# The last unit's weight sums in a scratch buffer, and one weight block split by VectorE instead of by an accumulating DMA

## The chip, the cores and the metric

The kernel runs on one core of one Trainium2 chip. The metric is the device time of one execution in microseconds (us). The core's engines are TensorE (PE, matmuls; its weight loads are listed as PEld), VectorE (DVE), ScalarE (ACT), GpSimd (POOL) and SyncE (SP, which only issues transfers here). POOL issues transfers too, above all those that add to their destination.

## What is computed

One layer of a decoder trunk on 1024 prompt tokens and 8 sample tokens (1032 columns), model width 1024: a mixer with pooling and convolution, cross attention, and a gated feed-forward block with 22 tiles of 128 hidden channels. The change lies in the last step, the down projection and the final norm:

```python
    h = rmsnorm(x, g_ffn)
    x = x + (jax.nn.silu(h @ w_gate) * (h @ w_up)) @ w_down
...
        y_prompt = rmsnorm(xp, g_final)
```

## The kernel before, around the change

**Two parts per factor.** Every matmul operand is kept as a high part and a low part, and each product is three passes (high by high, high by low, low by high). ScalarE, or GpSimd, makes the high part. The low part is made in one of two ways. In `split` (line 365) VectorE subtracts the high part from the raw tile. In `split_by_dma` (line 390) ScalarE writes the negated high part, and a transfer issued by GpSimd adds the raw data from memory to it a second time. The table `BY_DMA` (line 49) names the weight blocks that take the second way.

**The down projection.** The first 16 hidden tiles go through a scheme with seven products per 2x2 block (Strassen's, in Winograd's form). They make 4 chunks, and every chunk works on 4 pairs of output rows: 16 units, numbered `u` = 0 to 15 (`down(u)`, line 1538). A unit has seven products: three of 512 columns on plain weights `dW` (6 matmuls each), and four of 520 columns on weight sums `dV` (12 matmuls of 260 columns each). `dn_load(u)` (line 1490) fetches the unit's raw weights into a tile `dr`. `dn_prep(u)` (line 1494) forms four sums of quarters of `dr` in a tile `dt` (256 columns each, line 1506, on VectorE or GpSimd), splits `dt` into `dV`, and splits parts of `dr` into `dW`. The results are added to the residual `x2` and to partial sums `pp` by VectorE (line 1339). `second_half` (line 1575) combines them by VectorE at line 1347.

**The last six hidden tiles** (16 to 21) are multiplied plainly. `hidden_load` (line 1583) fetches each into a scratch tile `ht` and splits it by DMA into `ho`. The weights come as six blocks, in this order (line 415): `w_dn` 16, `w_dn2` 0, `w_dn` 17, `w_dn` 18, `w_dn2` 1, `w_dn` 19, each through a raw tile `raw` into `w`. `last_down(c, n)` (line 1648) makes the eight output tiles `fd` of a span `c` of columns, by 18 matmuls per tile and 512 or 2x260 columns: four hidden tiles with a `w_dn` block, then two with a `w_dn2` block. `fd_0` and `fd_1` use `w_dn` 16 and `w_dn2` 0, `fd_2` and `fd_3` use `w_dn` 17 and `w_dn2` 0, and so on.

**Buffers.** Raw tiles (`dr`, `dt`, `raw`) share 3 buffers with the tag `raw`; `ht` and other scratch tiles share 3 buffers with the tag `scr`; `w` has 2, and `op` has 19. A tile takes a buffer only when the last reader of its former tile is done.

**The order.** `Program.order` (line 146) sets it: a list planner with a cost for every task takes, again and again, the engine that can start first, and the task of highest priority that is ready there and has its buffers. What it decides is written out as one fixed sequence per engine. So a buffer's tag can change which task comes first on every engine.

Of the kernel before, what the change touches and what calls it, by code (L numbers as in the profile page):

```python
# [14 lines left out]
P = 128  # L15
D = 1024
# [30 lines left out]
)  # L47

BY_DMA = {"w_in": (3, 4, 6, 7, 9, 10, 11), "w_k": (2, 3, 5, 6), "w_o": (4, 5, 6), "w_out_a": (1,), "w_out_b": (3,), "w_q": (4, 5, 6), "w_v": (0, 7), "w_dn": (17, 18, 19), "w_dn2": (1,)}
WIDE = ("w_k", "w_v")  # L50
LEAD = {"w_k": 2, "w_v": 3, "w_out_a": 15, "w_q": 15, "w_in": 1, "w_out_b": 12, "w_o": 8}
LAST_SPANS = ((0, 512), (512, 260), (772, 260))
# [28 lines left out]
CHUNKS, FIRST_LAST = 4, 16  # L81
# [22 lines left out]
class Program:  # L104
# [10 lines left out]
    def add(self, engines, emit, r=(), w=(), lock=False, func=None, nbytes=0):  # L115
        t = Task()
        t.engines = {}
        for e, cost in engines.items():
            factor, more = self.margin.get(e, (1, 0)) if not nbytes else (1, 0)
            t.engines[e] = cost * factor + more  # L120
        t.emit, t.lock, t.func, t.nbytes = emit, lock, func, nbytes
        t.prio = len(self.tasks) + self.later
        if "PE" not in engines and any(isinstance(x[0], Buf) and x[0].tag in ("mm", "ms") for x in r):
            t.prio += BIAS["evac"]
        deps = set()
        for x in r:
            if x in self.writer:
                deps.add(self.writer[x])
        for x in w:
            if x in self.writer:  # L130
                deps.add(self.writer[x])
            deps.update(self.readers.get(x, ()))
        for x in r:
            self.readers.setdefault(x, []).append(t)
        for x in w:
            self.writer[x], self.readers[x] = t, []
        deps.discard(t)
        t.deps, t.followers, t.ends = deps, [], {}
        t.waiting = len(deps)
        for d in deps:  # L140
            d.followers.append(t)
        t.bufs = list({id(x[0]): x[0] for x in list(r) + list(w) if isinstance(x[0], Buf)}.values())
        self.tasks.append(t)
        return t
# [116 lines left out]
def hybrid_step_kernel(ctx: ExitStack, tc: tile.TileContext, io):  # L261
# [11 lines left out]
    def buf(name, tag, shape, dtype=F32):  # L273
        return Buf(name, tag, shape, dtype)

    def op_buf(name, shape=(P, 2, T), dtype=F32):
        return buf(name, "op", shape, dtype)

    def op_r(name, shape=(P, 2, T)):
        return buf(name, "op", shape, F32R)  # L280

    def scr(name, shape=(P, T)):
        return buf(name, "scr", shape)
# [26 lines left out]
    def dve(n):  # L310
        return 0.065 + 0.00105 * n

    def pool_tt(n):
        return 0.14 + 0.00216 * n
# [50 lines left out]
    def split(dst, key, src, n, r, gain=None, ps=False):  # L365

        hi = {"ACT": act(n, ps, gain is not None)}
        if not ps and not state.get("alone"):
            hi["Pool"] = pool_ts(n)

        def emit_hi(e):
            if e is nc.scalar:
                e.activation(dst(0), src(), AF.Copy, scale=1.0 if gain is None else gain)  # L373
            else:
                e.tensor_scalar(dst(0), src(), 1.0 if gain is None else gain, 1.0, ALU.mult, ALU.mult)

        add(hi, emit_hi, r, [key(0)])
        lo = {"DVE": dve(n)}
        if gain is None and not ps and not state.get("alone"):
            lo["Pool"] = pool_tt(n)  # L380

        def emit_lo(e):
            if gain is None:
                e.tensor_tensor(dst(1), src(), f32(dst(0)), ALU.subtract)  # L384
            else:
                e.scalar_tensor_tensor(dst(1), src(), gain, f32(dst(0)), ALU.mult, ALU.subtract)

        add(lo, emit_lo, list(r) + [key(0)], [key(1)], lock=not ps)

    def split_by_dma(dst, key, src, n, r, again, again_keys, pool_too=False):  # L390


        def scaled(e, p, src, factor):
            if e is nc.scalar:
                e.activation(dst(p), src, AF.Copy, scale=factor)
            else:
                e.tensor_scalar(dst(p), src, factor, 1.0, ALU.mult, ALU.mult)

        either = {"ACT": act(n), "Pool": pool_ts(n)} if pool_too else {"ACT": act(n)}
        add(either, lambda e: scaled(e, 0, src(), 1.0), r, [key(0)])  # L400
        add(either, lambda e: scaled(e, 1, f32(dst(0)), -1.0), [key(0)], [key(1)])
        add({"Pool": 0.6}, lambda e: e.dma_start(dst(1), again(), accum_op=ALU.add), [key(1)] + again_keys, [key(1)], nbytes=4 * P * n)
# [38 lines left out]
    def w_prep():  # L441
# [3 lines left out]
        w = buf(f"w{i}", "op" if name in WIDE or i >= len(seq) - 4 else "w", (P, 2, 1024), F32R)  # L445
        if j in BY_DMA.get(name, ()):
            split_by_dma(lambda p: w[:, p], lambda p: (w, p), lambda: raw[:], 1024, [(raw,)],
# [1021 lines left out]
    def later(work, bias="prep"):  # L1469
        pg.later = BIAS[bias]  # L1470
        work()
        pg.later = 0
# [2 lines left out]
    x2 = [op_buf(f"x2_{j}") for j in range(4)]  # L1475
    pp = [op_buf(f"pp{j}", (P, 4, TW)) for j in range(2)]
    dn_raw, dn_w, db = {}, {}, {}

    def quarter2(p, q):


        if q < 4:
            i, h = q // 2, q % 2
            return lambda sl=slice(0, HW[h]): x2[p][:, i, h * HALF + sl.start : h * HALF + sl.stop]
        return lambda sl=slice(0, TW): pp[p // 2][:, p % 2 * 2 + q - 4, sl]
# [6 lines left out]
        dma(lambda: dn_raw[u][:], lambda: io["w_dn"][u], 4 * P * D, w=[(dn_raw[u],)])  # L1492

    def dn_prep(u):
        raw, t = dn_raw[u], buf(f"dt{u}", "raw", (P, D))
        W, V = buf(f"dW{u}", "w", (P, 2, 768), F32R), op_r(f"dV{u}", (P, 2, 1024))
        dn_w[u] = W, V

        def b(half, i):
            return lambda: raw[:].rearrange("p (k i n) -> p k i n", k=4, i=2)[:, half::2, i]  # L1500

        def s(q):
            return lambda: t[:].rearrange("p (q j n) -> p q j n", q=4, j=2)[:, q]

        def minus(q, a, b, keys, op=ALU.subtract):
            add({"Pool": pool_tt(256), "DVE": dve(256)}, lambda e: e.tensor_tensor(s(q)(), a(), b(), op), keys, [(t, q)], lock=True)

        minus(0, b(0, 1), b(0, 0), [(raw,)])
        minus(2, s(0), b(1, 1), [(raw,), (t, 0)])
        minus(3, b(1, 1), b(0, 1), [(raw,)])  # L1510
        minus(1, b(1, 0), s(2), [(raw,), (t, 2)], ALU.add)
        split(lambda p: V[:, p], lambda p: (V, p), lambda: t[:], 1024, [(t, q) for q in range(4)])
        split(lambda p: W[:, p, :512].rearrange("p (k n) -> p k n", k=4), lambda p: (W, p, 0),
              lambda: raw[:].rearrange("p (k i n) -> p k i n", k=4, i=2)[:, :, 0], 512, [(raw,)])
        split(lambda p: W[:, p, 512:].rearrange("p (k n) -> p k n", k=2), lambda p: (W, p, 1), b(1, 1), 256, [(raw,)])

    def down_blocks(c, which):
        for b in which:
            n = WIDTH[b]
            t = scr(f"hs{c}_{b}", (P, 2, n))  # L1520
            again = lambda b=b, n=n: hb[c, b][:, :, :n]
            dma(lambda t=t: t[:], again, 8 * P * n, r=[("hb", c, b, j) for j in range(2)], w=[(t,)])
            o = db[c, b] = op_r(f"hb{c}_{b}", (P, 2, 2, n))
            part, key, src = (lambda p, o=o: o[:, p]), (lambda p, o=o: (o, p)), (lambda t=t: t[:])
            if c and b in DOWN_ORDER[:4]:
                split_by_dma(part, key, src, 2 * n, [(t,)], again, [("hb", c, b, j) for j in range(2)])
            else:
                split(part, key, src, 2 * n, [(t,)])
# [75 lines left out]
    for f in range(FF_TILES):  # L1604
        if f + 1 < FF_TILES:
            if f + 1 >= AHEAD:
                later(lambda: gu_load(f + 1), "load")
                later(lambda: gate_prep(f + 1))
            later(lambda: sums_prep(f + 1))
        else:  # L1610
            pg.margin = MARGINS["down"]
            later(lambda: dn_load(0), "load")
            later(lambda: dn_prep(0))
            later(lambda: down_blocks(0, DOWN_ORDER[:4]))
        if f < AHEAD:
            others(f)
        else:
            seven(f)
    later(lambda: residual_load(0))
    later(lambda: down_blocks(0, DOWN_ORDER[4:]))  # L1620
    units = 4 * CHUNKS
    for u in range(units):
        c, p = u // 4, u % 4
        if u + 1 < 4:
# [221 lines left out]
```

## Time and profile before

| what | value |
| --- | --- |
| median of 3 runs | 1228.38 us |
| lowest and highest of them | 1224.43 and 1228.46 us |
| the profiled execution, its own time | 1224.89 us |
| its span in the profile | 1223.0 us |
| granted TensorE clock over the span | 0.997 |

The profile is of one execution. Between its span and its own time lie 1.9 us outside the program's instructions. In rows of the profile, times are in us from the span's start, buffer numbers are left out of names, and `<-` after an idle time names what ended it. A line number can be that of a helper: 1323 is every product of the seven-product schemes, 384 every low part made by subtraction, 373 and 395 every high part.

### The profile page before, as it was taken

How to read it: one execution, taken by the hardware profiler on the slowest of the kernel's cores; microseconds unless marked ns; L12 is line 12 of the kernel's file. 1: busy time of each engine (PE TensorE's matmuls, PEld its weight loads, DVE VectorE, ACT ScalarE, POOL GpSimd, SP SyncE). 2: the span in 40 equal slices, each digit the busy share in tenths (PEclk: the TensorE clock that was granted, in tenths of full speed). 3: DMA queues.
4: the chain of work that ended last, by engine and by line, in shares of the span. 5: the costliest groups of instructions: out<-in, count | busy, mean ns of one | idle time of the engine just before them, and what ended most of it. 6: DMA issues, size and time to landing. Idle time of an engine off the chain costs nothing.

```text
span 1223.0 us, 19412 instructions
## 1 busy us (share of the span) xinstructions
PE 1200.1 (98%) x7720; PEld 1122.0 (92%) x7720; DVE 927.2 (76%) x1549; ACT 527.8 (43%) x722; POOL 243.3 (20%) x296
## 2 busy tenths in 40 slices
PE   8999999999999999999999999999999999999997
PEld 8999988999999979989999999999999999999786
DVE  7999999767258886679777777777867788888654
ACT  7765556455134533444222322233222365545433
POOL 3568841231111102111000000000000124332101
PEclk9999999999999999999999999999999999999998
DMA  7335678226395773421232233222313698668612
GB/s 287 86 72 114 143 210 250 105 104 194 115 294 182 240 280 103 156 104 61 104 113 79 96 113 113 105 78 96 122 70 111 217 317 239 172 183 220 155 50 90
DMA packets 60875, 181.80 MB, mean 149 GB/s; under 512 B 7857, under 2 KB 11633, under 8 KB 59505
## 3 DMA queue, kind: packets, MB, share of 16 engines
q1 hardware_dynamic: 53824, 157.92, 37.1%
q0 software_dynamic: 6960, 22.65, 10.5%
q8 instruction: 60, 0.98, 0.3%
q14 instruction: 31, 0.25, 0.1%
HBM read 146.76 MB, written 33.78 MB: 148 GB/s over the span
## 4 chain that ended last, share of the span: by engine, by line
PE 76%; DVE 4%; DMA 2%; issue 2%; ACT 1%; POOL 0%; DVEq 0%; POOLq 0%; ACTq 0%
PE pr L1323 48%; PE ps L480 7%; PE po L480 7%; PE fd L1665 5%; PE ob L480 4%; PE oa L480 3%; PE sc L1023 1%; PE pv L1081 1%; DMA w<-in_w_q 1%; DMA raw<-in_w_out_a 1%; DMA w<-in_w_dn 0%; DVE spcache_k L1120 0%; DMA spcache_k<-in_cache_k 0%; DVE oo L1086 0%; DVE pT L1067 0%
## 5 line engine op out<-in xcount | busy, mean ns | idle before, releaser
L1323 PEld LDWEIGHTS pr<-ab,wTb 128*128 128x128 f32 x1056 | 132.1, 188 | 3.6
L1323 PE MATMUL pr<-ab,wTa 128*128 128x260 f32 x1056 | 133.6, 282 | 0.0
L1323 PE MATMUL pr<-ab,wTb 128*128 128x260 f32 x1056 | 133.3, 282 | 0.0
L1323 PEld LDWEIGHTS pr<-ab,wTa 128*128 128x128 f32 x1056 | 130.7, 189 | 2.0 <-DVE su L1339 0.3
L1323 PE MATMUL pr<-ab,wG 128*128 128x512 f32 x528 | 128.8, 392 | 0.0
L1339 DVE TENSOR_TENSOR su<-pr,su 128x520 f32<-128x520 f32 (+1 forms) x112 | 77.5, 694 | 57.5 <-PE pr L1323 57.3
L480 PE MATMUL ps<-xop,w 128*128 128x344 f32 x720 | 114.1, 320 | 0.0
L480 PEld LDWEIGHTS ps<-xop,w 128*128 128x128 f32 x720 | 113.6, 188 | 0.0
L1323 PEld LDWEIGHTS pr<-ab,wG 128*128 128x128 f32 x528 | 96.3, 188 | 18.8
L1323 PEld LDWEIGHTS pr<-hb,dV 128*128 128x128 f32 x768 | 98.4, 188 | 5.8 <-ACT dV L373 0.9
L1323 PE MATMUL pr<-hb,dV 128*128 128x260 f32 x768 | 100.2, 283 | 1.0 <-DVE dV L384 0.5
L480 PE MATMUL ps<-xq,w 128*128 128x344 f32 x576 | 94.8, 321 | 0.3 <-DMA w<-in_w_q 0.3
L480 PEld LDWEIGHTS po<-oo,w 128*128 128x128 f32 x576 | 90.9, 188 | 0.6 <-DVE oo L1086 0.4
L480 PE MATMUL po<-oo,w 128*128 128x344 f32 x576 | 91.4, 320 | 0.0
L480 PEld LDWEIGHTS ps<-xq,w 128*128 128x128 f32 x576 | 90.7, 188 | 0.7 <-DMA w<-in_w_q 0.6
L684 DVE SCALAR_TENSOR_TENSOR cacc<-glu,vec,cacc 128x511 f32<-128x511 f32 (+14 forms) x116 | 76.9, 739 | 0.0
L1323 PE MATMUL pr<-hb,dW 128*128 128x512 f32 x288 | 74.2, 394 | 0.0
L1665 PE MATMUL fd<-ho,w 128*128 128x260 f32 (+1 forms) x432 | 69.8, 322 | 0.7 <-DMA w<-in_w_dn 0.6
L1665 PEld LDWEIGHTS fd<-ho,w 128*128 128x128 f32 x432 | 61.7, 188 | 8.4 <-DMA w<-in_w_dn 1.1
L373 ACT ACTIVATE w<-raw 128x1024 fp32r<-128x1024 f32 (+1 forms) x35 | 32.9, 944 | 77.1 <-issue 19.7
L1323 PE MATMUL pr<-ab,wU 128*128 128x512 f32 x264 | 64.8, 394 | 0.0
L1350 POOL MEMSET su<- 128x16 f32 x22 | 2.5, 111 | 310.0 <-PE pr L1323 244.3
(306 smaller groups left out, 2183.9 us busy)
## 6 DMA issues: line engine op xcount, KB each, us to landing
gr<-in_w_gu SPq DMA_DIRECT2D x44, 512.0 KB, 3.6
hb<-su SPq DMA_DIRECT2D x8, 1040.0 KB, 4.6
hs<-hb SPq DMA_DIRECT2D x16, 520.0 KB, 6.7
dr<-in_w_dn SPq DMA_DIRECT2D x16, 512.0 KB, 3.7
spcache_k<-in_cache_k SPq DMA_DIRECT2D x12, 512.0 KB, 5.2
hs<-hb SPq DMA_DIRECT2D x12, 512.0 KB, 4.7
raw<-in_w_in SPq DMA_DIRECT2D x10, 512.0 KB, 3.7
hb<-he SPq DMA_DIRECT2D x8, 520.0 KB, 3.2
```

The source lines that it names most:

```text
L373: e.activation(dst(0), src(), AF.Copy, scale=1.0 if gain is None else gain)
L480: e.matmul(ps[:, c, :CW], w[:, wi, cols], x[:, xi, c * CW : (c + 1) * CW], start=first and p == 0, stop=last and p == 2)
L684: e.scalar_tensor_tensor(acc[h][:, n:], src[:, : HALF - n], w, acc[h][:, n:], ALU.mult, ALU.add)
L1023: e.matmul(bank()[:, i * NMEM : (i + 1) * NMEM], qop[2 * h + dt][:, qi, tt * P : (tt + 1) * P], kk[:, ki, 2 * (h % 2) + dt], start=(dt == ...
L1081: e.matmul(ps[:, c], v[:, vi, m, col : col + P], pT[h][m][:, pi, sl], start=(m == 0 and p == 0), stop=(m == 1 and p == 2))
L1323: e.matmul(bank(c), w[:, wi, cols(j)], xs[0](j, xi)[:, c * n : (c + 1) * n], start=onto is None and j == 0 and p == 0, stop=j == nj - 1 an ...
L1339: from_sums(sums, "DVE", dve, lambda e, src, sl: e.tensor_tensor(as_banks(o(sl), src), src, as_banks(a(sl), src), op), [akey], [okey])
L1350: add({"Pool": 0.12}, lambda e: e.memset(o(), 0.0), [], keys)
L1665: e.matmul(view(i), w[:, wi, col : col + P], hops[k][:, xi, half, lo - half * HALF + i * width // count : lo - half * HALF + (i + 1) * wid ...
```

## The change

Three edits. The block `w_dn` 17 leaves the table `BY_DMA`, so its low part is made by VectorE (`split`) and not by a negated copy and an adding transfer (`split_by_dma`). The sums `dt` of the last unit, `u` = 15, take a scratch buffer instead of a raw one. The line `units = 4 * CHUNKS` moves up, and all lines behind it are numbered one higher.

```diff
-BY_DMA = {"w_in": (3, 4, 6, 7, 9, 10, 11), "w_k": (2, 3, 5, 6), "w_o": (4, 5, 6), "w_out_a": (1,), "w_out_b": (3,), "w_q": (4, 5, 6), "w_v": (0, 7), "w_dn": (17, 18, 19), "w_dn2": (1,)}
+BY_DMA = {"w_in": (3, 4, 6, 7, 9, 10, 11), "w_k": (2, 3, 5, 6), "w_o": (4, 5, 6), "w_out_a": (1,), "w_out_b": (3,), "w_q": (4, 5, 6), "w_v": (0, 7), "w_dn": (18, 19), "w_dn2": (1,)}
...
     dn_raw, dn_w, db = {}, {}, {}
+    units = 4 * CHUNKS
...
     def dn_prep(u):
-        raw, t = dn_raw[u], buf(f"dt{u}", "raw", (P, D))
+        raw, t = dn_raw[u], scr(f"dt{u}", (P, D)) if u == units - 1 else buf(f"dt{u}", "raw", (P, D))
...
     later(lambda: down_blocks(0, DOWN_ORDER[4:]))
-    units = 4 * CHUNKS
+
     for u in range(units):
```

The planner answers with another order near the end; up to unit 12 the engines' sequences stay as they were. Three places matter later.

On TensorE, from the first product of unit 15 (`dW_10685` before, `dW_10689` now; `dV_10841` and `dV_10621` are its sums, `w_10805` and `w_10817` before are `w_dn` 16 and `w_dn2` 0). Before:

```order
L1323 MATMUL pr_10784<-hb_4_10066,dW_10685 128x512 x6
L1323 MATMUL pr_10797<-hb_2_10419,dW_10685 128x512 x6
L1323 MATMUL pr_10784<-hb_0_10183,dW_10685 128x512 x6
L1665 MATMUL fd_1_10821<-ho_10491,w_10805 128x512 x3
L1665 MATMUL fd_1_10821<-ho_10512,w_10805 128x512 x3
L1665 MATMUL fd_1_10821<-ho_10698,w_10805 128x512 x3
L1665 MATMUL fd_1_10821<-ho_10599,w_10805 128x512 x3
L1665 MATMUL fd_1_10821<-ho_10766,w_10817 128x512 x3
L1665 MATMUL fd_1_10821<-ho_10791,w_10817 128x512 x3
L1323 MATMUL pr_10856<-hb_3_10096,dV_10841 128x260 x12
```

Now:

```order
L1323 MATMUL pr_10790<-hb_4_10066,dW_10689 128x512 x6
L1323 MATMUL pr_10802<-hb_3_10096,dV_10621 128x260 x12
L1323 MATMUL pr_10820<-hb_5_10285,dV_10621 128x260 x12
L1323 MATMUL pr_10790<-hb_0_10183,dW_10689 128x512 x6
L1323 MATMUL pr_10849<-hb_6_10401,dV_10621 128x260 x12
L1323 MATMUL pr_10865<-hb_2_10419,dW_10689 128x512 x6
L1323 MATMUL pr_10876<-hb_1_10430,dV_10621 128x260 x12
L1666 MATMUL fd_0_10896<-ho_10504,w_10786 128x512 x3
```

Unit 15's four products on sums stood behind `fd_1`, and now they stand among its plain products, with all of `fd` behind them. `fd_0` and `fd_1` then run in turns: four hidden tiles each with `w_dn` 16, then two each with `w_dn2` 0 (`w_10890`).

On GpSimd, the last sums and adding transfers before:

```order
L402 DMA ho_10599<-hd 128x1040
L402 DMA ho_10698<-hd 128x1040
L402 DMA ho_10766<-hd 128x1040
L402 DMA ho_10791<-hd 128x1040
L1506 TENSOR_TENSOR dt_10819<-dr_10526,dt_10819 128x256
L402 DMA w_10869<-in_w_dn 128x1024
L402 DMA w_10906<-in_w_dn 128x1024
L402 DMA w_10925<-in_w_dn 128x1024
L402 DMA w_10945<-in_w_dn 128x1024
```

Now:

```order
L1507 TENSOR_TENSOR dt_10568<-dr_10520 128x256
L1507 TENSOR_TENSOR dt_10568<-dt_10568,dr_10520 128x256
L1507 TENSOR_TENSOR dt_10568<-dr_10520,dt_10568 128x256
L402 DMA ho_10517<-hd 128x1040
L402 DMA ho_10599<-hd 128x1040
L402 DMA ho_10702<-hd 128x1040
L402 DMA ho_10797<-hd 128x1040
L402 DMA ho_10816<-hd 128x1040
L402 DMA w_10873<-in_w_dn 128x1024
L402 DMA w_10910<-in_w_dn 128x1024
L402 DMA w_10930<-in_w_dn 128x1024
```

GpSimd makes three sums of unit 15 (`dt_10568`) where it made one (`dt_10819`). They stand ahead of the second hidden tile's adding transfer instead of behind the sixth's, and the four adding transfers for weights are three.

On VectorE, now, from the sixth product of unit 12 (`pr_10559`) on; `dr_10520` is the raw tile of unit 15, `dt_10541` holds the sums of unit 14:

```order
L1339 TENSOR_TENSOR x_0_9109<-pr_10559,x_0_9109 128x512
L1507 TENSOR_TENSOR dt_10568<-dr_10520 128x256
L1347 TENSOR_TENSOR x_0_9109<-x_0_9109 128x512
L1339 TENSOR_TENSOR x_0_9109<-pr_10572,x_0_9109 128x520
L1339 TENSOR_TENSOR x_1_9087<-pr_10592,x_1_9087 128x512
L1347 TENSOR_TENSOR x_0_9109<-x_0_9109,pp_9095 128x512
L384 TENSOR_TENSOR dV_10570<-dt_10541,dV_10570 128x1024
```

Before, VectorE's three sums of unit 15 stood far behind this, after the low part of `w_dn` 16. Now its one sum of `dr_10520` stands ahead of the first result of unit 13 (`pr_10592`).

## The prediction, written before the changed kernel had run

> **What bounds the kernel now.** First the page's busy times.
>
> ```profile
> span 1223.0 us, 19412 instructions
> PE 1200.1 (98%) x7720; PEld 1122.0 (92%) x7720; DVE 927.2 (76%) x1549; ACT 527.8 (43%) x722; POOL 243.3 (20%) x296
> ```
>
> TensorE is busy 98% of the span, so no edit that leaves its work alone can gain more than its waits. Next TensorE's timeline near the end, from unit 14 on, since the change acts there:
>
> ```profile
> 1122.08 3.06 PE L1323 MATMUL pr<-hb,dV 128*128 128x260 f32 x24
> 1124.97 1.56 PE L1323 MATMUL pr<-hb,dW 128*128 128x512 f32 x6
> ...
> 1130.64 4.32 PE L1323 MATMUL pr<-hb,dW 128*128 128x512 f32 x18
> 1134.79 4.75 PE L1665 MATMUL fd<-ho,w 128*128 128x512 f32 x18
> 1140.02 0.76 PE L1323 MATMUL pr<-hb,dV 128*128 128x260 f32 x4 [0.49 <-ACT dV L373]
> 1141.28 5.57 PE L1323 MATMUL pr<-hb,dV 128*128 128x260 f32 x44 [0.51 <-DVE dV L384]
> 1146.69 4.79 PE L1665 MATMUL fd<-ho,w 128*128 128x512 f32 x20
> 1152.12 10.22 PE L1665 MATMUL fd<-ho,w 128*128 128x512 f32 x43 [0.63 <-DMA w<-in_w_dn]
> ```
>
> In its brackets three waits are named, of 0.49, 0.51 and 0.63 us. These are too short, because the modelled end of a matmul covers part of each, so I measure them by the starts. Without a wait, 18 matmuls of 512 columns go from 1130.64 to 1134.79, or 0.2306 us each, and 24 of 260 go from 1122.08 to 1124.97, or 0.1204 us each. At these rates `fd_1` would end at 1134.79 + 18 x 0.2306 = 1138.94, but the next start is at 1140.02: 1.08 lost. Four matmuls lead to 1140.50, the next is at 1141.28: 0.78. Then 44 lead to 1146.58, the next is at 1146.69: 0.11. Then 20 lead to 1151.30, the next is at 1152.12: 0.82. Together **2.79 us** are lost between the start of unit 15 and `fd_2`.
>
> The timeline of all engines tells what was late:
>
> ```profile
> 1134.21 1.22 DVE L384 TENSOR_TENSOR w<-raw,w 128x1024 fp32r<-128x1024 f32 x1
> ...
> 1137.07 1.81 POOL L1506 TENSOR_TENSOR dt<-dr,dt 128x256 f32<-128x256 f32 x1 [5.21 <-issue]
> 1137.07 1.21 DVE L384 TENSOR_TENSOR w<-raw,w 128x1024 fp32r<-128x1024 f32 x1
> 1138.21 1.23 DVE L1347 TENSOR_TENSOR x<-x,pp 128x520 f32<-128x520 f32 x1
> ...
> 1138.91 5.20 SPq L359 DMA_DIRECT2D raw<-in_w_dn  x4
> 1138.91 1.06 ACT L373 ACTIVATE dV<-dt 128x1024 fp32r<-128x1024 f32 x1 [2.86 <-POOL dt L1506]
> 1140.00 1.23 DVE L384 TENSOR_TENSOR dV<-dt,dV 128x1024 fp32r<-128x1024 f32 x1 [0.57 <-ACT dV L373]
> ...
> 1142.69 1.06 ACT L395 ACTIVATE w<-raw 128x1024 fp32r<-128x1024 f32 x1 [2.72 <-DMA raw<-in_w_dn]
> ...
> 1146.28 0.87 POOL L402 DMA_DIRECT2D w<-in_w_dn  x1 [7.41 <-ACT w L395]
> ```
>
> All three raw buffers were taken: unit 15's weights, `w_dn` 16, `w_dn2` 0. The sums of unit 15 could start only when the low part of `w_dn` 16 (VectorE, 1134.21 to 1135.43) freed one. Their last piece ends on GpSimd at 1138.88, and `dV`'s high and low parts follow at 1138.91 and 1140.00, each with TensorE behind it. `w_dn` 17 could be fetched only when unit 15's raw tile was free, at 1138.91. Then came its conversion (1142.69), a negated copy, and the adding transfer (1146.28), whose landing TensorE met at 1152.12.
>
> **The scratch buffer.** The edit removes this knot: the sums no longer wait for a raw buffer. They wait for unit 15's weights. SP issues these, in both orders after the third hidden tile's load is out and when the same VectorE instruction frees the buffer, at
>
> ```profile
> 1104.30 0.33 SPq L359 DMA_DIRECT2D dr<-in_w_dn  x1
> ```
>
> How long that takes beside an adding transfer is bounded by these tiles, first `raw` (SP), then `ho` (adding, GpSimd), minimum, median and maximum:
>
> ```profile
> DMA to landing us min/median/max: 4.3/5.7/7.1
> ...
> DMA to landing us min/median/max: 5.5/6.9/10.1
> ```
>
> I take 5.7, an SP transfer of the same size: the weights are there at 1110.0, with 7.1 at 1111.4, and 10.1 (1114.4) is the far end. The sums on GpSimd cost 0.73 to 1.81 each:
>
> ```profile
> L1506 POOL TENSOR_TENSOR dt<-dr x3: 732/749/1737, 1093.5 to 1106.5; 128x256 f32<-128x256 f32 x3
> L1506 POOL TENSOR_TENSOR dt<-dr,dt x3: 731/800/1808, 1096.7 to 1137.1; 128x256 f32<-128x256 f32 x3
> ```
>
> Even at 1114.4, three of 1.81, 1.06 for the high and 1.23 for the low part end at 1122.1 on their own. TensorE wants them at 1130.64 + 6 x 0.2306 = 1132.02, ten us later. So 1.08 + 0.78 + 0.11 = **1.97 us** go, if nothing else becomes late. What lies behind is due earlier than before. Unit 15 now runs without a stop, 18 x 0.2306 + 48 x 0.1204 = 9.93, to 1140.57. After 24 matmuls with `w_dn` 16 come, at 1146.10, `w_dn2` 0 and the fifth hidden tile, and at 1146.80 the sixth. `fd_2` starts at 1148.87.
>
> - *Hidden tiles five and six.* ScalarE converts them only when unit 14's last matmul frees an operand buffer, at 1130.64. Four passes of 1.06 take 4.2:
>
> ```profile
> 1100.45 1.06 ACT L395 ACTIVATE ho<-ht 128x1040 fp32r<-128x1040 f32 x1
> ```
>
>  So GpSimd issues the adding transfers at about 1132.9 and 1135.0. With the median 6.9 the second lands at 1141.9, with 10.1 at 1145.1, and it is due at 1146.80: the cover is 1.7 to 4.9 us. I take no cost.
> - *`w_dn2` 0.* ScalarE's order has its high part behind that of `w_dn` 18, whose fetch starts when `w_dn` 16 is split, near 1134.3. With 7.1 it lands at 1141.4. Then 1.06 and 1.06 on ScalarE and 1.22 on VectorE lead to 1144.8, and the low part is due at 1146.10 + 2 x 0.2306 = 1146.56. With 10.1 it comes 1.2 us late. I take none.
>
> **`w_dn` 17 by VectorE.** This removes a second pass on ScalarE like that of 1142.69 (1.06), 0.87 of GpSimd's issue, and an adding transfer that TensorE met 5.8 us after its issue. It adds one subtraction of 1.22 us to VectorE. Its raw tile is fetched before unit 15 begins, since the sums hold no raw buffer. ScalarE reaches it at about 1134.9, right behind the hidden tiles, and the low part is there near 1137.3. Due at 1148.87, it has 11 us, so the **0.82 us** at 1152.12 go too. The added 1.22 us stand in VectorE's queue ahead of two results of unit 15, the second of which (`pr_10849`) leaves the buffer that `fd_0` takes at 1140.57. TensorE ends it at 1130.64 + 12 x 0.2306 + 36 x 0.1204 = 1137.74, VectorE adds it in 0.69, by 1138.6: two us of cover. Without them the subtraction would cost up to its 1.22. The remaining three adding transfers start near 1144, and with 10.1 the first lands at 1154, due at `fd_4`, 1148.87 + 36 x 0.2306 = 1157.2.
>
> **The sum:** -1.97 - 0.82 = -2.79, nothing added. That is -2.8 us on the profiled execution's own 1224.89, or 1222.1.
>
> **A rule against it.** By the Trainium skill, page "SBUF — State Buffer", section "Who interferes with whom", a VectorE instruction with two SBUF inputs and a GpSimd instruction that reads SBUF lock each other out for a whole instruction. The trace agrees: GpSimd's sum at 1137.07 took 1.81 against 0.73, and VectorE's combination at 1138.21 took 1.23 (the one at 1112.01, quoted below, has 0.68). By this rule the three sums on GpSimd cost up to 1.1 us more each, which the ten us above cover; it raises the chance of the second rival.
>
> **The rivals.** *One of the two late pieces takes the wait's place* (hidden tile six or `w_dn2` 0). For it speaks that both chains start only after unit 14 or `w_dn` 16, against it that it takes landings of the slowest kind. Price 1.2 us: the gain shrinks to 1.6, 1223.3 on the profiled execution.
>
> *VectorE stands for unit 15's weights*, and the kernel becomes slower. Its one sum of `dr` now stands ahead of the first result of unit 13, in a stretch where VectorE has nothing to spare:
>
> ```profile
> 1090.00:1100.00 10.00, 10.00 (x68) 9.19 (x67) 9.71 (x13) 6.28 (x8) 3.88 (x4) 1.00 0.38 113
> 1100.00:1110.00 10.00, 10.00 (x69) 9.22 (x68) 8.94 (x14) 5.09 (x7) 4.00 (x5) 1.00 0.94 270
> 1110.00:1120.00 10.00, 10.00 (x69) 9.23 (x68) 9.11 (x15) 4.00 (x7) 0.87 (x1) 1.00 0.97 245
> ```
>
> (the fourth column is VectorE's busy time, the last but one the DMA share). Unit 13 starts two units of 9.93 before 1130.64, at 1110.78, and TensorE adds to that first result after 18 of its matmuls, at 1110.78 + 6 x 0.2306 + 12 x 0.1204 = 1113.61. Behind the sum VectorE has 0.34, twice 0.61 and 0.69 to do (results start 0.61 apart in 1111.40, 1112.01):
>
> ```profile
> 1111.40 0.69 DVE L1339 TENSOR_TENSOR x<-pr,x 128x520 f32<-128x520 f32 x1
> 1112.01 0.68 DVE L1347 TENSOR_TENSOR x<-x,pp 128x512 f32<-128x512 f32 x1
> ```
>
> So weights that land after 1111.36, 7.1 us after their issue, stop TensorE. The median 5.7 is clear of that, 7.1 is at the edge, and 10.1 costs 3.0. Since VectorE is busy 27.8 of 30 us here, I add half a microsecond for a locked combination (1.23 - 0.68): +3.5 - 2.8 = +0.7, 1225.6. The sign turns at a landing 9.4 us after the issue. Against it: with the order now, only one adding transfer is under way then, since the second hidden tile's stands behind the sums on GpSimd.
>
> *The change doesn't do what it says*: the scratch buffer holds back the loads of hidden tiles, and the sixth comes so late that the knot only moves. VectorE frees the sums' buffer behind the fifth result of unit 13, which ends at 1110.78 + 12 x 0.2306 + 36 x 0.1204 = 1117.88. With 0.69 and 1.23 the load goes out at 1119.8, SP's 7.1 gives 1126.9, and ScalarE can use it near 1132.8. I see little for this; of the gain only `w_dn` 17's 0.8 would be left, 1224.1.
>
> **How the numbers follow.** The forecast, all waits gone, 0.70; a late piece 0.15; VectorE's stand 0.10; the knot moves 0.05. The runs shown spread from 1224.43 to 1228.46, and the profiled execution, 1224.89, lies near their lowest, 3.5 below their median. Minus 2.8 gives 1222.1 from the one and 1225.6 from the other; nothing in the profile says where in such a spread the next median falls, so I state the middle, **1223.8**. The range goes from 1221.0, the lowest run less 2.8 and 0.6 of scatter, to 1228.0, which holds every rival but VectorE's stand reckoned from the median (1229.1). Half a per cent of 1228.38 is 6.1 us, about what a measurement of this kernel can tell from no change. Faster than that means below 1222.2: the forecast, with a median near the low end of the spread, 0.70 x 0.5 x 0.7 = 0.25, and a little for scatter, 0.28. Slower than 1234.5 takes VectorE's stand several times over, 0.04. Within it: 0.68.
>
> **What would show it.** In the profile after, TensorE's timeline should run from the first product of unit 15 to `fd_2` with no idle time named, 18 + 48 + 36 matmuls in 18.2 us. The waits for `dV` and for `w` from `w_dn` should be gone from the list, SP's fetch of `w_dn` 17 should lie before 1130, and the last GpSimd sum near 1113. A wait of TensorE near 1113, or of VectorE on `dr`, speaks for the second rival; one at 1146, for `ho` or `w`, for the first. The forecast is wrong if TensorE's waits after 1100 sum to more than 1.5 us, or if time went elsewhere than between 1100 and 1153.

## The result, and the profile after

| | changed | before |
| --- | --- | --- |
| median of 12 runs | 1221.01 us | 1224.81 us |
| lowest and highest | 1219.22 and 1224.36 us | 1222.53 and 1232.47 us |
| ratio, 95% interval | 0.9962 [0.9948, 0.9976] | |
| the profiled execution, its own time and its span | 1222.57 and 1220.7 us | 1224.89 and 1223.0 us |

The changed kernel is faster: by 3.8 us between the medians, and by the ratio 4.7 us of 1224.81, with an interval from 2.9 to 6.4. That is less than half a per cent, and clear of zero. Among the experiments' runs of the kernel before are two slow ones, of 1680.20 and 2392.16 us; the medians below hold them, the ratios do not.

The page's busy times hardly move (with 19409 instructions, 3 fewer):

```profile
PE 1196.9 (98%) x7720; PEld 1121.0 (92%) x7720; DVE 927.7 (76%) x1549; ACT 527.3 (43%) x721; POOL 242.0 (20%) x296
```

TensorE has the same 7720 matmuls in 3.2 us less of modelled busy time, and ScalarE one instruction fewer, the negated copy.

TensorE's timeline of the changed kernel, from unit 15's first product on (start, length, operation, count; a wait would stand in brackets at the end):

```profile
1131.26 1.55 PE L1323 MATMUL pr<-hb,dW 128*128 128x512 f32 x6
1132.64 3.03 PE L1323 MATMUL pr<-hb,dV 128*128 128x260 f32 x24
1135.52 1.54 PE L1323 MATMUL pr<-hb,dW 128*128 128x512 f32 x6
1136.89 1.60 PE L1323 MATMUL pr<-hb,dV 128*128 128x260 f32 x12
1138.34 1.53 PE L1323 MATMUL pr<-hb,dW 128*128 128x512 f32 x6
1139.70 1.60 PE L1323 MATMUL pr<-hb,dV 128*128 128x260 f32 x12
1141.14 37.08 PE L1666 MATMUL fd<-ho,w 128*128 128x512 f32 x174
1178.06 1.02 PE L1697 MATMUL fin_ps<-fin,ones_d 128*128 128x512 f32 x2
```

No bracket is left. `fin_ps`, the first matmul of the final norm, is in both kernels the next landmark behind the same TensorE work. Before, it stood here:

```profile
1180.39 1.02 PE L1696 MATMUL fin_ps<-fin,ones_d 128*128 128x512 f32 x2
```

From unit 15's first product to `fin_ps` I call **the stage**. It took 1180.39 - 1130.64 = 49.75 before, and takes 1178.06 - 1131.26 = 46.80 now: **2.95 us less**. The span fell by 2.3 only, because this profile reached unit 15 0.62 later, on work that the change left alone.

The other engines of the changed kernel, first VectorE's timeline:

```profile
1111.04 0.43 DVE L1507 TENSOR_TENSOR dt<-dr 128x256 f32<-128x256 f32 x1 [0.21 <-DMA dr<-in_w_dn]
1111.38 1.23 DVE L1347 TENSOR_TENSOR x<-x 128x512 f32<-128x512 f32 x1
...
1136.69 1.23 DVE L384 TENSOR_TENSOR w<-raw,w 128x1024 fp32r<-128x1024 f32 x1 [0.28 <-ACT w L373]
...
1143.11 1.23 DVE L384 TENSOR_TENSOR w<-raw,w 128x1024 fp32r<-128x1024 f32 x1
```

Then SP's and GpSimd's:

```profile
1104.96 0.33 SPq L359 DMA_DIRECT2D dr<-in_w_dn  x1
...
1125.39 0.33 SPq L359 DMA_DIRECT2D raw<-in_w_dn  x1
```

```profile
1113.30 0.73 POOL L1507 TENSOR_TENSOR dt<-dr,dt 128x256 f32<-128x256 f32 x1
...
1136.01 0.86 POOL L402 DMA_DIRECT2D ho<-hd  x1 [1.22 <-ACT ho L395]
```

Unit 15's weights were issued at 1104.96, and VectorE stood 0.21 for them, until 1111.04. The last sum ends on GpSimd at 1114.03, where it ended at 1138.88 before. `w_dn` 17 is fetched at 1125.39 and no longer at 1138.91, its low part is ready at 1137.92, and that of `w_dn2` 0 at 1144.34.

### The profile page after: what moved, and what is told of

It reads as the page before. It is cut to its first block, busy times and chain, and to the rows that moved or that the text cites. A ratio compares the mean times of both kernels' runs of the same rounds, so it can differ in the third digit from the quotient of the medians.

```text
span 1220.7 us, 19409 instructions
## 1 busy us (share of the span) xinstructions
PE 1196.9 (98%) x7720; PEld 1121.0 (92%) x7720; DVE 927.7 (76%) x1549; ACT 527.3 (43%) x721; POOL 242.0 (20%) x296
## 4 chain that ended last, share of the span: by engine, by line
PE 76%; DVE 4%; DMA 3%; issue 2%; ACT 0%; DVEq 0%; SPq 0%; ACTq 0%; POOLq 0%
PE pr L1323 47%; PE po L480 7%; PE fd L1666 6%; PE ps L480 5%; PE oa L480 4%; PE ob L480 4%; PE sc L1023 1%; DMA dr<-in_w_dn 1%; DVE spcache_k L1120 1%; DMA spcache_k<-in_cache_k 1%; PE pv L1081 1%; DMA w<-in_w_k 1%; PE kps L850 0%; DMA sbcache_k<-qd 0%; DVE oo L1086 0%
```

## The experiments

Theory A at the start: the raw buffer held by unit 15's sums made all of the loss in the stage, `w_dn` 17's late fetch too, and the scratch buffer alone gains it. Theory B: the scratch buffer gains the 1.97 us ahead of `fd_2`, and `w_dn` 17 by VectorE the 0.82 behind it, as the prediction had it. The later runs ask what covers each freed wait, and how large the gain is. Each was compared with runs of the kernel before on the same chip.

### e1_scratch_only: the scratch buffer alone

```diff
-"w_dn": (18, 19)
+"w_dn": (17, 18, 19)
```

(in `BY_DMA` of the changed kernel, so `w_dn` 17 takes the adding transfer again.)

> Sums of unit 15 in a scratch buffer, w_dn 17 still by the adding transfer. Theory A (every bit of the gain is TensorE's waits between the start of unit 15 and fd_2, and the raw buffer alone caused them all, since w_dn 17 is fetched some 14 us earlier when the sums hold no raw buffer): as the full change, no wait of TensorE there, -2.9 us against before, and 89.4 us from unit 15's first product to the end of the span. Theory B (the sum of the prediction, each edit its own term): -2.0, with a wait of about 0.8 for w_dn 17 left in front of fd_2, 90.3 us.

Median 1222.37 beside 1225.12, ratio 0.9966 [0.9946, 0.9986]. TensorE's timeline, and GpSimd's issue for `w_dn` 17:

```profile
1134.47 1.55 PE L1323 MATMUL pr<-hb,dW 128*128 128x512 f32 x6
...
1144.36 37.08 PE L1666 MATMUL fd<-ho,w 128*128 128x512 f32 x174
1181.28 1.02 PE L1697 MATMUL fin_ps<-fin,ones_d 128*128 128x512 f32 x2
```

```profile
1141.26 0.86 POOL L402 DMA_DIRECT2D w<-in_w_dn  x1 [1.18 <-ACT w L395]
```

The stage takes 1181.28 - 1134.47 = 46.81, the changed kernel's to 0.01. The adding transfer goes out at 1141.26 for a block due at 1144.36 + 36 x 0.2306 = 1152.66: that is 11.4 us, where TensorE was there 5.8 us after the issue before. TensorE's sequence is that of the changed kernel, instruction for instruction. Theory A holds, and B falls.

### e2_dve_only: `w_dn` 17 by VectorE alone

```diff
-"w_dn": (17, 18, 19)
+"w_dn": (18, 19)
```

(in `BY_DMA` of the kernel before.)

> w_dn 17 split by VectorE, the sums of unit 15 still in a raw buffer. Both theories: the wait of 0.8 in front of fd_2 goes, the waits for dV stay, 91.5 us from unit 15's first product to the end (92.4 before). Theory A adds that the fetch of w_dn 17 stays behind unit 15's sums, near 1139, and that VectorE's added 1.22 us stand near unit 15's results, where they may give 0.2 back: -0.6 to -0.8 us against before.

Median 1223.54 beside 1225.12, ratio 0.9983 [0.9966, 1.0001]. TensorE:

```profile
1129.67 4.32 PE L1323 MATMUL pr<-hb,dW 128*128 128x512 f32 x18
...
1139.06 0.74 PE L1323 MATMUL pr<-hb,dV 128*128 128x260 f32 x4 [0.49 <-ACT dV L373]
1140.32 4.13 PE L1323 MATMUL pr<-hb,dV 128*128 128x260 f32 x32 [0.51 <-DVE dV L384]
1144.60 1.72 PE L1323 MATMUL pr<-hb,dV 128*128 128x260 f32 x12 [0.15 <-DVE x L1339]
...
1178.94 1.02 PE L1696 MATMUL fin_ps<-fin,ones_d 128*128 128x512 f32 x2
```

The stop for `w_dn` 17 is gone and both for `dV` stay. A new one comes ahead of 1144.60, where VectorE was late with a product's result. The stage is 49.27, 0.5 less than before. So this edit is not empty: alone it removes 0.9 and gives back some 0.4. With the scratch buffer there is nothing left for it to remove.

### e3_before_again, e4_after_again, e10_after_third, e11_before_third: both kernels unchanged

> The kernel before, unchanged, against itself: how far two equal kernels come apart. Theory A (the measured -3.8 is -2.9 and scatter): a ratio within 0.25% of 1 and not always at it, and a start of unit 15 that lies within 1 us of 1130.6 with the 92.4 us behind it unchanged to 0.1. Theory C (a further 0.9 us is gained ahead of unit 15): the start of unit 15 agrees with that of before to 0.2 and lies later than in every profile of the changed kernel.

> The changed kernel again. Theory A: -2.9 us within the interval, 89.4 us from unit 15's first product to the end, start of unit 15 anywhere within 1 us of 1130.6. Theory C: -3.8 and a start of unit 15 earlier by 0.9 than that of before on this chip.

> The changed kernel a third time, for the size of the gain: 46.8 us from unit 15's first product to the final norm's first matmul, as in the profiles before, and a ratio to before of 0.9976 within its interval (-2.9 us) if the two ratios of 0.9962 were that and scatter; another 0.9962 with an interval below 0.9976 if a further 0.9 us is gained elsewhere.

> The kernel before against itself once more, beside the run above: ratio 1 within its interval, 49.7 us from unit 15's first product to the final norm's first matmul. The changed kernel's ratio over this one's is the size of the gain.

| kernel | median | before beside it | ratio, 95% interval |
| --- | --- | --- | --- |
| before, e3 | 1223.92 | 1225.12 | 0.9994 [0.9973, 1.0016] |
| before, e11 | 1223.52 | 1224.64 | 0.9989 [0.9972, 1.0006] |
| changed, e4 | 1221.06 | 1225.12 | 0.9962 [0.9944, 0.9981] |
| changed, e10 | 1221.19 | 1224.64 | 0.9974 [0.9959, 0.9990] |

TensorE of e3, then of e4:

```profile
1129.58 4.32 PE L1323 MATMUL pr<-hb,dW 128*128 128x512 f32 x18
...
1179.23 1.02 PE L1696 MATMUL fin_ps<-fin,ones_d 128*128 128x512 f32 x2
```

```profile
1128.39 1.55 PE L1323 MATMUL pr<-hb,dW 128*128 128x512 f32 x6
...
1175.19 1.02 PE L1697 MATMUL fin_ps<-fin,ones_d 128*128 128x512 f32 x2
```

The stage is 49.65 and 46.80, and in e11 and e10 it is 49.77 and 46.80: it repeats to 0.1 us. When unit 15 begins does not: 1130.64, 1129.58 and 1131.23 for the kernel before, 1131.26, 1128.39 and 1129.21 for the changed one. So theory C, a further 0.9 us ahead of unit 15, is not borne out. Theory A's guess of a start within 1 us of 1130.6 missed too, by 2.2 in e4. The medians of the pairs sent together differ by 2.86 (e4 and e3) and 2.33 (e10 and e11), which is the stage's gain. The larger figures against the runs beside them (4.06 and 3.45 by medians) hold 1.1 to 1.2 us by which the unchanged kernel came out lower too. Why it did so both times is open; its own intervals hold 1.

### e5_late_weights: unit 15's weights fetched twice

SP first fetches unit 14's weights to the same place, so that the right ones land late.

```diff
-        dma(lambda: dn_raw[u][:], lambda: io["w_dn"][u], 4 * P * D, w=[(dn_raw[u],)])
+        def emit(e):
+            if u == units - 1:
+                e.dma_start(dn_raw[u][:], io["w_dn"][u - 1])
+            e.dma_start(dn_raw[u][:], io["w_dn"][u])
+
+        add({"SP": 0.05}, emit, (), [(dn_raw[u],)], nbytes=4 * P * D)
```

> The changed kernel with unit 15's raw weights fetched twice, one fetch after the other, so that they land later; nothing else moves. In the profile after, they were issued at 1104.96 and landed 5.95 later, and VectorE waited 0.21 for them at 1111.04; its sum must start by 1111.94 there, or TensorE stops in front of the second half of unit 13's first product. The second rival of the prediction: they land 3.7 to 6 us later than in the profile after, VectorE stands that long, TensorE stops for 2.9 to 5.0 us near 1114, and the gain is gone: within 1 us of the time before, or over it. Its opposite (VectorE's queue has slack that takes the stand up): TensorE stops for less than 1 us, and the gain stays above 2.

Median 1225.86 beside 1223.71, ratio 1.0021 [1.0003, 1.0040]: slower than before. SP, VectorE, then TensorE:

```profile
1103.09 0.33 SPq L1495 DMA_DIRECT2D dr<-in_w_dn  x1
1108.65 0.33 SPq L1496 DMA_DIRECT2D dr<-in_w_dn  x1
```

```profile
1112.66 0.42 DVE L1512 TENSOR_TENSOR dt<-dr 128x256 f32<-128x256 f32 x1 [3.70 <-DMA dr<-in_w_dn]
1113.00 1.21 DVE L1347 TENSOR_TENSOR x<-x 128x512 f32<-128x512 f32 x1
```

```profile
1109.51 1.53 PE L1323 MATMUL pr<-hb,dW 128*128 128x512 f32 x6
1110.88 1.60 PE L1323 MATMUL pr<-hb,dV 128*128 128x260 f32 x12
1115.48 2.33 PE L1323 MATMUL pr<-hb,dW 128*128 128x512 f32 x6 [3.00 <-DVE x L1339]
1117.61 3.97 PE L1323 MATMUL pr<-hb,dV 128*128 128x260 f32 x24
1121.41 1.53 PE L1323 MATMUL pr<-hb,dW 128*128 128x512 f32 x6
...
1124.23 1.55 PE L1323 MATMUL pr<-hb,dW 128*128 128x512 f32 x6
```

The weights were there 9.6 us after the first issue, VectorE stood for them, the combination behind its sum took 1.21 beside GpSimd's sums, and TensorE, due at 1110.88 + 12 x 0.1204 = 1112.32, went on at 1115.48: a stop of 3.16. That is the second rival's chain, link by link. But unit 13 took 1124.23 - 1109.51 = 14.72, not 9.93: 4.8 more, not 3.2. The rest lies behind the stop. By stretch (stretch, length, TensorE's busy time, weight loads, VectorE, ScalarE, GpSimd, then granted clock, DMA share, GB/s):

```profile
1115.50:1117.60 2.10, 2.10 (x6) 1.64 (x7) 2.10 (x3) 1.06 (x1) 1.80 (x3) 0.67 0.26 34
1117.60:1119.00 1.40, 1.40 (x8) 1.39 (x7) 1.40 (x3) 0.00 (x0) 0.00 (x0) 0.50 0.97 152
1119.00:1121.40 2.40, 2.40 (x19) 2.40 (x19) 1.17 (x3) 0.00 (x0) 0.00 (x0) 0.87 1.06 197
```

The granted clock fell to half: 0.67 over the first stretch means 1.4 us of half clock in it, 0.87 over the third 0.6 us, with the second 3.4 us in all. The 30 matmuls from 1115.48 to 1121.41 took 5.93 where 6 x 0.2306 + 24 x 0.1204 = 4.27 is normal: 1.66 more. By the Trainium skill, page "TensorE: Matmul & The Clock Gate", section "Part 1: The HAM clock gate (the "warmup" mystery)", the clock goes to half after an idle window of about 3.4 us, which runs freely, and returns after about 3.4 us of work. The trace agrees on the 3.4 us of half clock, but not on the idle: 3.16 us were enough here, and 1.80 us in a stop that e9's profile shows.

### e9_late_by_less: the same with a quarter of the first fetch

```diff
-                e.dma_start(dn_raw[u][:], io["w_dn"][u - 1])
+                e.dma_start(dn_raw[u][:, :256], io["w_dn"][u - 1][:, :256])
```

> As the run with unit 15's weights fetched twice, but the first fetch takes only 256 of 1024 columns, so that the whole lands some 8 us after the first issue instead of 9.5. There TensorE stopped for 3.15 us, and its granted clock then fell to half for 3.4 us, which cost 1.7 more; VectorE's stand ended 7.0 us after the issue plus that stop, 0.55 of it a locked combination. If the stop follows the landing and the clock falls only after a stop of some 3 us: a stop of 0.5 to 2 us, and unit 13 lasts 9.9 us plus the stop alone. If every stop costs clock: unit 13 lasts longer than that by 0.5 or more. In time: after plus the stop, still faster than before by 1 to 2.4 us.

Median 1223.86 beside 1224.64, ratio 0.9993 [0.9975, 1.0011]. TensorE's timeline, one of its stretches with the columns as above, then SP and VectorE:

```profile
1114.73 1.54 PE L1323 MATMUL pr<-hb,dW 128*128 128x512 f32 x6
1116.10 1.60 PE L1323 MATMUL pr<-hb,dV 128*128 128x260 f32 x12
1119.53 1.68 PE L1323 MATMUL pr<-hb,dW 128*128 128x512 f32 x6 [1.83 <-DVE x L1339]
1121.04 3.06 PE L1323 MATMUL pr<-hb,dV 128*128 128x260 f32 x24
...
1126.76 1.55 PE L1323 MATMUL pr<-hb,dW 128*128 128x512 f32 x6
```

```profile
1119.50:1127.00 7.50, 7.47 (x50) 6.91 (x51) 7.45 (x11) 2.04 (x4) 1.86 (x3) 1.00 0.79 154
```

```profile
1108.31 0.33 SPq L1495 DMA_DIRECT2D dr<-in_w_dn  x1
...
1116.70 0.43 DVE L1512 TENSOR_TENSOR dt<-dr 128x256 f32<-128x256 f32 x1 [2.51 <-DMA dr<-in_w_dn]
```

Landed 8.4 us after the first issue, the weights stopped TensorE from 1117.54 to 1119.53, 2.0 us. The clock stays at 1.00, and unit 13 takes 12.03, 2.1 more: the stop and 0.1 for the restart (six matmuls from 1119.53 to 1121.04 in 1.51, not 1.38). Most of the gain is gone, but not all.

That a stop of some 2 us leaves the clock alone is no rule. Some 570 us earlier, at six matmuls that no edit touched, e9's TensorE (first line) and that of the kernel before (second) stood for the same 1.80 us:

```profile
549.24 3.80 PE L510 MATMUL Rf_ps<-xss,ones_d 128*128 128x512 f32 x6 [1.80 <-DVE xss L411]
546.28 2.32 PE L510 MATMUL Rf_ps<-xss,ones_d 128*128 128x512 f32 x6 [1.80 <-DVE xss L411]
```

In e9 the granted clock was 0.51 from 549.50 to 552.90, and the six matmuls took 1.48 us longer; in the kernel before it was 1.00. So the length of a stop does not settle by itself whether half clock follows.

### e6_op_buffer: the sums in an operand buffer

```diff
-scr(f"dt{u}", (P, D)) if u == units - 1
+op_buf(f"dt{u}", (P, D)) if u == units - 1
```

> The sums of unit 15 in one of the 19 operand buffers instead of a scratch buffer. If all that counts is that they hold no raw buffer: the same stage as after, 46.8 us from unit 15's first product to the first matmul of the final norm (49.7 before), and -2.9 us. If the scratch buffer matters as such (its hidden loads moved): a stage of its own, different by over 0.3.

Median 1221.53 beside 1223.71, ratio 0.9989 [0.9963, 1.0015]. TensorE:

```profile
1129.32 1.55 PE L1323 MATMUL pr<-hb,dW 128*128 128x512 f32 x6
...
1143.26 33.47 PE L1666 MATMUL fd<-ho,w 128*128 128x512 f32 x158 [0.18 <-DMA ho<-hd]
1176.57 1.02 PE L1697 MATMUL fin_ps<-fin,ones_d 128*128 128x512 f32 x2
```

The stage is 47.25. Nearly all of the gain comes with this buffer too, which is not raw either; what it gives back, 0.45, is a stop for a hidden tile's adding transfer. That is the first rival's kind of wait, at a third of its price. It comes with another order: here TensorE runs `fd_0` over all six hidden tiles before `fd_1`, so the sixth is due at 1139.21 + 16 x 0.2306 = 1142.90, and its transfer goes out only 8.8 us before:

```profile
1134.07 0.86 POOL L402 DMA_DIRECT2D ho<-hd  x1 [1.21 <-ACT ho L395]
```

The slowest of these landings took 9.1 us in this profile. The ratio by itself tells this kernel neither from the changed one nor from the one before.

### e7_all_by_dve: no weight of the last step by an adding transfer

```diff
-"w_dn": (18, 19), "w_dn2": (1,)
+"w_dn": (), "w_dn2": ()
```

> The changed kernel with the last three blocks (w_dn 18, w_dn2 1, w_dn 19) split by VectorE too: three subtractions of 1.22 us more, three adding transfers and three ScalarE passes fewer. VectorE is busy 11.2 of 20 us there, and each block is due 8 us after the one before. Cover theory: no wait of TensorE, the stage stays 46.8. Rival (VectorE's results of fd come late behind the subtractions, so that a bank is not free): a wait of up to 1.2 per block, a stage of 47 to 50.

Median 1221.46 beside 1223.71, ratio 0.9981 [0.9966, 0.9995]. In its profile no wait of TensorE is named from 1000 us to the final norm, and the stage is 46.80. Three more subtractions on VectorE cost nothing there, as the cover said, and gain nothing: the transfers that they replace were hidden.

### e8_all_sums_scratch: the sums of all 16 units in scratch buffers

```diff
-scr(f"dt{u}", (P, D)) if u == units - 1 else buf(f"dt{u}", "raw", (P, D))
+scr(f"dt{u}", (P, D))
```

> The sums of all 16 units in scratch buffers. The loads of the next chunk's blocks need the same 3 buffers and were fetched one chunk ahead, so some of them now go out late: waits of TensorE in front of units of the middle chunks, 2 to 6 us in all, slower than the changed kernel by that, the stage from unit 15 on still 46.8. Rival (scratch buffers stand free there): the same time as the changed kernel.

Median 1223.99 beside 1223.71, ratio 1.0007 [0.9984, 1.0029]. The stage keeps its 46.8, and a new stop appears in TensorE's timeline in unit 4:

```profile
1025.12 1.66 PE L1323 MATMUL pr<-hb,dW 128*128 128x512 f32 x6 [1.00 <-DVE x L1339]
```

That is less than the 2 to 6 us expected in the profile. By the ratio no gain is to be seen, and one stop of 1.00 us does not account for that; where the rest went is open. No run shows a gain from moving the other units' sums.

## Where the prediction was right, and where it failed

**The main mechanism was right.** A raw buffer was what the sums waited for, and the waits named for `dV` and `w_dn` 17 are gone, and none is named from 1100 to the final norm. The stage lost 2.95 between the first two profiles and 2.85 between e3's and e4's. The sum had 2.79. The 0.16 that it lacked stands in two places. Unit 15 runs in 1141.14 - 1131.26 = 9.88, not 9.93. And behind the last stop the pace is lost for a moment: from 1152.12 to `fin_ps` the kernel before took 28.27, while the changed one needs for the same matmuls 36.92 - 38 x 0.2306 = 28.16, so 0.11 more than the brackets and starts up to 1152.12 can show. e9's restart shows the same 0.1 at another stop.

**The scratch buffer.** The weights were there 6.1 us after their issue, where the sum took 5.7 and gave 7.1 as the point from which TensorE stops. The sums were finished at 1114.03 (forecast near 1113), 18 us before the first product on them.

**The covers held.** The sixth hidden tile's transfer was issued at 1136.01 (forecast 1135.0 plus 0.62 for the later unit). The landings of these tiles in the changed kernel were

```profile
DMA to landing us min/median/max: 5.6/6.1/9.3
```

so even the slowest is there at 1145.3, due at 1146.80 + 0.62 = 1147.4. `w_dn2` 0 was ready at 1144.34, for 1147.2. e6's stop of 0.45 us does not speak against this cover: there the sixth tile was due 8.8 us after its issue, and here it is due 11.4 us after, later than any landing of these tiles took (10.1 at most, in the kernel before).

**The step that failed: 0.82 us for `w_dn` 17 by VectorE.** The prediction wrote that its own subtraction removes this stop. e1 removes it without that edit. The prediction had the reason in hand: `w_dn` 17 "could be fetched only when unit 15's raw tile was free", and the scratch buffer frees that one as well. The earlier fetch serves the adding transfer as much as the subtraction. The right terms are 2.95 for the scratch buffer and nothing for VectorE's subtraction behind it; e2 shows that the subtraction alone is worth 0.5. That the total of 2.79 came out near is luck as far as the split goes: both edits were in the kernel.

**The second rival's point was right, its price was not.** A landing of 7.1 us as the edge and 3.5 for 10.1 us came from a stop alone. e9 (8.4 after the issue) gave 2.0 where 8.4 - 7.1 + 0.5 = 1.8 was to be expected, and e5 (9.6) a stop of 3.16 where 3.0 was. But in e5 the half clock added 1.7 behind the stop, so a landing near 10 us cost about five there, not 3.5. The sign turns between 8.4 and 9.6 us; the forecast of 9.4 lies between them, though it stood on the stop alone.

**The stated time failed on its base.** "Nothing in the profile says where in such a spread the next median falls, so I state the middle, 1223.8": the median of before is 1224.81 over 12 runs, the three shown among them. It lies on the profiled execution's 1224.89, and not midway from there to 1228.38, at 1226.6, which the stated time took as its base. That base was 1.8 too high, the larger part of the 2.8 by which 1223.8 missed. Against 1224.81 the stated time meant a gain of 1.0 only, where the medians differ by 3.8. From the profiled execution the forecast was 1222.1. The result of 1221.01 lies at the low edge of the range. Of the three runs two agreed at 1228.4, and yet the lone one at 1224.4 was the typical one.

**"About what a measurement of this kernel can tell from no change" was too coarse.** The interval of the ratio is 0.14% to each side, not 0.5%. The gain does stay within half a per cent, as the likeliest case said, but it is no tie.

**What stays open.** The ratio's 4.7 us is more than the stage's 2.95, which is just inside its interval. Up to unit 12 the engines' sequences are the same in both kernels, the start of unit 15 scatters over 8 us between profiles of all kernels (1128.39 in e4, 1136.70 in e9, whose unit 13 cost only 2.1 of it), and the pairs sent together give 2.3 and 2.9. Part of the scatter is to be seen in stops of TensorE far ahead of the edits: 3.47 us ahead of 36.45 in e1 and of 36.75 in e9, where the kernel before stood 0.21, and 2.79 us ahead of 200.48 in e7. So I hold 2.9 us for the effect; that the rest is chance is argued, not shown. Nor does any run move the sums to another buffer and keep the engines' old order, so the free buffer and the order that the planner made with it count as one cause here.

## What to carry to other kernels

When several late pieces stand one behind the other, ask for each what it waited for before giving it a price: here one held buffer delayed sums, fetch and transfer, and moving a single small tile out of that pool freed all three, while the edit aimed at the last piece gained nothing more. Size a microsecond's effect from a stage between two landmarks of the trace, which repeated to 0.1 us, and take the base for the stated time from enough runs, since three of them missed the median by 3.6. Price a stop of an otherwise busy TensorE with its restart, and reckon that half clock can follow it: here it did behind one of 3.16 us and one of 1.80 us, but not behind one of 2.0 us.

## What the runs showed of the hardware

- A stop of 3.16 us brought 3.4 us at half clock (0.50 granted) and cost 1.7 us beyond itself (e5). In e9 one of 1.80 us brought it too (0.51, 1.5 us beyond itself), and one of 2.0 us did not; the same stop of 1.80 us brought none in the kernel before. What decides beside the length is open.
- After a stop at full clock, the next six matmuls took 1.51 us in e9 instead of 1.38, which the named wait does not contain.
- A VectorE combination took 1.21 to 1.23 us while GpSimd was at its sums, in the kernel before (1138.21), the changed one (1111.38) and e5 (1113.00), against 0.68 for one at 1112.01 in the kernel before.
